# A written order for the first stage of a hybrid decoder block

## The chip, the cores and the metric

The kernel runs on one core of a Trainium2 chip. The metric is the device time of one execution in microseconds (us); lower is better. The engines are TensorE (PE: matmuls, with PEld for its weight loads), VectorE (DVE), ScalarE (ACT), GpSimd (POOL) and SyncE (SP, which here only issues DMAs). Each engine takes its instructions in the order of its own list and waits on semaphores.

## The reference

One decoder block over 1024 tokens of width 1024 in float32. The part that matters here is the beginning:

```python
cond = silu(c)
sh1, sc1, g1, sh2, sc2, g2 = split(cond @ w_ada + b_ada, 6)
h = rmsnorm(x, norm1_g) * (1 + sc1) + sh1
u, q, k, v, gate_a, gate_b = split(h @ w_in)
y_a = s5_branch(u, lam_re, lam_im, log_dt, b_re, b_im, c_re, c_im, d_skip, w_glu, b_glu) @ w_a
y_b = stick_breaking_attention(q, k, v) @ w_b
x = x + g1 * ((sigmoid(gate_a) * y_a + sigmoid(gate_b) * y_b) @ w_o)
# then a second norm and modulation, a SwiGLU FFN of width 2816, and a last norm
```

The S5 branch is a state-space recurrence with complex diagonal states: from `lam`, `log_dt`, `b` and `c` it derives powers of `exp(lam*dt)`, scaled input matrices and output matrices before any token is touched.

## The kernel before, in words

Matmuls with full precision are made of three products: each operand is split into a high half (float32r) and a low half (the rest), and high x high, high x low and low x high are summed (`PRODUCTS`). A weight tile is loaded into a staging tile (`ws` or `wgs`), its high half is cast on ScalarE and its low half is a subtraction on another engine. The halves live in a ring of buffers (`wring`: `wh`/`wl` with two buffers each, used by two of the three entries, and `wgh`/`wgl` with one); `self.turn` counts which entry is next.

The function `start` (L509 to L608) is the first stage. It computes u = h @ w_in[:, 0:512], transposed, in two halves of 512 tokens:

- `load` (L543) fetches four x tiles of 128 tokens and squares them on ScalarE; `half` (L527) computes 1/rms, scales the four tiles (one on ScalarE, one on GpSimd, two on VectorE), transposes them on TensorE column block by column block and copies each block to `xT` on ScalarE.
- `ada(g)` (L552) loads half of the shift and half of the scale columns of w_ada, multiplies them with the conditioning vector on TensorE (`ada_mm`, L860, four products side by side in strips of 32 rows), adds up the strips with a product by ones (L567), and loads and splits two of the four w_in tiles (`u_weight`; low halves on GpSimd, L425).
- `modulate(k, h)` (L575) makes the high half of a modulated column block on ScalarE (L578), the full value on VectorE (L579) and the low half on GpSimd (L580).
- `product` (L589) and `store` (L591): 96 products for each half of the tokens; a store copies a finished block on ScalarE and writes it to `uD` in DRAM. The store buffers `us` are three.
- `small` (L492) loads the small parameter rows on SP's queue and turns them into columns. The class `S5` computes all its parameters in one function, `params` (L78 to L197), on VectorE, with its loads on SP and ScalarE's queue.

After `start` the S5 recurrence (`inject`, `phases`, `outputs`, `run`) runs on VectorE and TensorE beside `v_proj` (L640, product L651) and eight blocks of `gate` (product L630), whose matmuls fill TensorE. `s5.run` waits for u from DRAM. The memory of the first stage's pools is used again by that stage.

The order of instructions on each engine is not written out: a planner (`schedule_with_timeline_sim=True`) simulates the program with its own costs and takes, on each engine, what is ready, earlier program text first. `self.after` and `keep_in_program_order` pin single instructions.

Of the kernel before, what the change touches and what calls it, by code (L numbers as in the profile page):

```python
# [9 lines left out]
F32 = mybir.dt.float32  # L10
F32R = mybir.dt.float32r
# [17 lines left out]
class S5:  # L29


    def __init__(self, tc, pool, work, psum, ident, lam_reT, lam_imT, log_dtT, b_re, b_im, c_re, c_im, d_skip):

        self.tc, self.nc = tc, tc.nc
        self.pool, self.work, self.psum, self.ident = pool, work, psum, ident
        self.params(lam_reT, lam_imT, log_dtT, b_re, b_im, c_re, c_im, d_skip)
# [41 lines left out]
    def params(self, lre, lim, ldt, b_re, b_im, c_re, c_im, d_skip):  # L78
        nc, pool, work = self.nc, self.pool, self.work
        v = nc.vector  # L80
        i = [0]

        def tmp():
            i[0] += 1
            return work.tile([128, 16], F32, name="tmp", bufs=24)
# [4 lines left out]
        tt(th, lim, dt, ALU.mult)  # L90
        self.vexp(r, ar, tmp)
# [5 lines left out]
        reduce(n, th)  # L97

# [8 lines left out]
        tt(w, ph, ph, ALU.mult)  # L107
        ts(s, w, 1.0 / math.factorial(13), None, ALU.mult)
# [6 lines left out]
        ts(c, c, 1.0, None, ALU.add)  # L115
        s2 = an
# [26 lines left out]

        nr, d, zr, zi, q = tmp(), tmp(), tmp(), tmp(), tmp()
# [15 lines left out]
        tt(zi, zi, d, ALU.mult)  # L160

        br, bi, t1, t2 = (work.tile([128, 16, 16], F32, name=k, bufs=1) for k in ("br", "bi", "bt1", "bt2"))
        nc.sync.dma_start(out=br, in_=b_re.rearrange("o (r g) p i -> (o g p) r i", g=2))
        nc.sync.dma_start(out=bi, in_=b_im.rearrange("o (r g) p i -> (o g p) r i", g=2))
# [19 lines left out]
        for srcs, dst in (((c_re, c_im), self.C), ((c_im, c_re), self.Cs)):  # L184
            cl = work.tile([128, 4, 2, 64], F32, name="cl", bufs=2)
            for k, src in enumerate(srcs):
                nc.scalar.dma_start(out=cl[:, :, k], in_=src.rearrange("o (t g) i p -> (o g i) t p", t=4))
# [4 lines left out]
        dsk = pool.tile([32, 16], F32, name="dsk")  # L192
        nc.scalar.dma_start(out=dsk, in_=d_skip.rearrange("o g i -> (o g) i"))
        self.dT = pool.tile([16, 32], F32, name="dT")
        ps = self.psum.tile([128, 512], F32, name="tp")
        nc.tensor.transpose(ps[0:16, 0:32], dsk, self.ident[0:32, 0:32])
# [143 lines left out]
P = 128  # L340
# [55 lines left out]
class Block:  # L396
# [94 lines left out]

    def small(self, const, pp):  # L492

        nc, i = self.nc, self.i
        rows = const.tile([P, P], F32, name="rows")
        ld = const.tile([16, 2], F32, name="ld")
        nc.gpsimd.memset(rows, 0.0)
        for a, n, k in ((64, "b_ada", 48), (48, "norm1_g", 8), (56, "norm2_g", 8), (112, "b_glu", 4)):
            nc.sync.dma_start(out=rows[a:a + k], in_=i[n].rearrange("o (k p) -> (o k) p", p=P))
        nc.sync.dma_start(out=ld, in_=i["log_dt"].rearrange("o (a b) -> (o a) b", b=2))  # L500
        nc.vector.tensor_copy(rows[0:16].rearrange("p (a b) -> p a b", a=2), ld.unsqueeze(2).broadcast_to([16, 2, 64]))
        nc.sync.dma_start(out=rows[16:32], in_=i["lam_re"].rearrange("o (a b) p -> (o a) (b p)", b=2))
        nc.sync.dma_start(out=rows[32:48], in_=i["lam_im"].rearrange("o (a b) p -> (o a) (b p)", b=2))
# [5 lines left out]
    def start(self, const, up, s5p):  # L509

        nc, i = self.nc, self.i
        ss = const.tile([P, KT], F32, name="ss1")
        x_v = i["x"].rearrange("o (t p) d -> p (o t) d", p=P)
        w_v = i["w_ada"].rearrange("o (p k) n -> (o p) k n", k=KT)
        self.hT = [[self.PA.tile([P, 2, 512], F32R, name="pa") for _ in range(KT)], []]
# [912 lines left out]
```

## Time and profile before

| | |
|---|---|
| three runs | 1528.68, 1532.48, 1535.25 us |
| median | 1532.48 us |
| span of the profiled execution, first to last instruction | 1530.4 us |
| TensorE busy in the span | 1409.0 us (92%) |
| VectorE busy | 1072.2 us (70%) |
| ScalarE, GpSimd busy | 614.0 us, 663.2 us |
| end of the last u product | 102.1 us |

The profiled execution's own time is known as its span alone; it lies 2.1 us under the median of the timed runs. In the views below, PE, PEld, DVE, ACT, POOL and SP are engines, a `q` behind a name is its sequencer issuing a DMA, L589 is line 589 of the kernel. A row of a timeline has the start in us, the duration in us, engine, line, operation, output <- input, partitions x elements, a count, and in brackets the idle time before it with what ended it. A row of the chain has start, duration, and engine with line, or a DMA. In the rows by stretches, each engine has busy us and (x instructions); then come TensorE's granted clock, the DMA engines' share and GB/s.

### The profile page before, as it was taken

The numbers are of one execution on the slowest core, as the hardware profiler recorded it, in microseconds if no ns is written. First come the engines' busy times: TensorE is split into PE (matmuls) and PEld (weight loads), VectorE is DVE, ScalarE is ACT, GpSimd is POOL, SyncE is SP. The second block draws the span as 40 slices with busy tenths as digits, with TensorE's granted clock in tenths as the row PEclk, the third lists the DMA queues.
The fourth block names the chain that finished last, engine by engine and source line by source line (L and its number), as shares of the span: only waits on it lengthen the run. The fifth ranks groups of instructions, "written<-read, shape, count | busy, mean of one in ns | idle before, by whom it ended". The sixth has DMA issues, their size and how long they took to land.

```text
span 1530.4 us, 18295 instructions
## 1 busy us (share of the span) xinstructions
PE 1409.0 (92%) x6578; PEld 1107.5 (72%) x6578; DVE 1072.2 (70%) x1443; ACT 614.0 (40%) x800; POOL 663.2 (43%) x369
## 2 busy tenths in 40 slices
PE   4898999996999898969799889999999998999995
PEld 2588888785666565638688668888888887788774
DVE  4658895555677776657624897666666758999998
ACT  5431122712566555655306543333333324343323
POOL 2520000102355557443410126445445459788795
PEclk9899999999999999989899999999999999999998
DMA  8556655498133234227423324333333146555312
GB/s 265 183 136 165 169 141 159 130 287 283 52 114 105 81 99 144 85 96 238 161 101 130 106 69 161 105 106 104 103 104 104 58 145 258 158 159 161 109 54 110
DMA packets 180962, 210.46 MB, mean 138 GB/s; under 512 B 29124, under 2 KB 122408, under 8 KB 180872
## 3 DMA queue, kind: packets, MB, share of 16 engines
q1 hardware_dynamic: 169800, 201.29, 41.5%
q10 hardware_dynamic: 11072, 8.00, 1.8%
q8 instruction: 52, 0.85, 0.2%
q14 instruction: 38, 0.31, 0.1%
HBM read 159.18 MB, written 48.89 MB: 136 GB/s over the span
## 4 chain that ended last, share of the span: by engine, by line
PE 45%; DVE 19%; DMA 12%; issue 10%; POOL 9%; ACT 4%; SPq 1%; ACTq 0%; POOLq 0%; DVEq 0%
PE tq L1143 12%; PE wo L1143 9%; PE wo L1024 5%; PE gu L1143 3%; PE mm L589 3%; PE mm L704 2%; POOL wa L806 2%; PE ga L630 2%; PE mx L704 2%; POOL wh L773 1%; PE mx L630 1%; POOL pb L1203 1%; DMA aw<-in_w_ada_dram 1%; DVE wa L802 1%; DVE acc L875 1%
## 5 line engine op out<-in xcount | busy, mean ns | idle before, releaser
L441 POOL TENSOR_TENSOR ws<-wb 128x1024 f32<-128x1024 f32 x26 | 64.2, 2471 | 192.0 <-PE tq L1046 90.1
L806 POOL TENSOR_TENSOR wa<-wa,wb 128x1024 f32<-128x1024 f32 (+2 forms) x32 | 80.6, 2519 | 73.5 <-DVE wa L802 49.3
L774 DVE TENSOR_TENSOR wl<-ws,wh 128x1024 fp32r<-128x1024 f32 (+1 forms) x40 | 52.7, 1317 | 67.1 <-POOL wh L773 67.1
L425 POOL TENSOR_TENSOR wl<-ws,wh 128x1024 fp32r<-128x1024 f32 x14 | 38.9, 2780 | 136.8 <-ACT wh L422 136.3
L807 ACT ACTIVATE wa<-wa 128x1024 f32<-128x1024 f32 (+1 forms) x40 | 38.9, 971 | 82.2 <-POOL wa L806 81.1
L1196 POOL TENSOR_TENSOR pa<-pa,row 128x1024 f32<-128x1024 f32 x22 | 66.0, 3023 | 1.8 <-DMA pa<-in_w_ffn_down_dram 1.8
L441 POOL TENSOR_TENSOR wgs<-wb 128x1024 f32<-128x1024 f32 x14 | 34.7, 2477 | 73.1 <-DVE wgl L444 30.5
L772 DVE SCALAR_TENSOR_TENSOR ws<-wa,ws 128x1024 f32<-128x1024 f32 (+1 forms) x40 | 53.4, 1335 | 13.0 <-ACT ws L771 12.6
L773 POOL TENSOR_SCALAR wh<-ws 128x1024 fp32r<-128x1024 f32 (+1 forms) x40 | 38.4, 959 | 54.1 <-DVE ws L772 52.8
L1134 POOL TENSOR_TENSOR f<-f,f 128x512 f32<-128x512 f32 x30 | 50.0, 1693 | 26.9 <-DVE f L1124 18.4
L704 PE MATMUL mm<-wa,V 128*64 128x512 f32 (+3 forms) x192 | 40.7, 517 | 21.5 <-ACT wa L807 21.4
L422 ACT CAST wh<-ws 128x1024 fp32r<-128x1024 f32 x28 | 29.2, 1048 | 61.5 <-PE wo L1024 32.9
L769 ACT ACTIVATE ws<-wa 128x1024 f32<-128x1024 f32 (+1 forms) x40 | 38.7, 968 | 30.3 <-DVE wa L766 29.8
L704 PE MATMUL z<-q,k 64*128 64x512 f32 (+3 forms) x192 | 42.6, 535 | 8.9 <-DVE gst L958 8.9
L875 DVE SCALAR_TENSOR_TENSOR acc<-aw,cond,acc 128x512 f32<-128x512 f32 x56 | 43.8, 782 | 9.9 <-DMA aw<-in_w_ada_dram 9.4
L1123 ACT ACTIVATE f<-f 128x1024 f32<-128x1024 f32 x22 | 23.4, 1061 | 60.9 <-DVE f L1163 31.0
L802 DVE TENSOR_TENSOR wa<-wa,acc 128x512 f32<-128x512 f32 (+1 forms) x80 | 46.6, 616 | 1.1 <-PE acc L704 1.1
L1225 POOL TENSOR_TENSOR wb<-pa 128x512 f32<-128x512 f32 x23 | 40.2, 1756 | 15.6 <-DVE wxl L1223 5.5
L273 POOL MEMSET tz<- 128x1024 f32 x4 | 3.8, 953 | 92.8 <-PE s5a L329 84.9
L1134 POOL TENSOR_TENSOR f<-f 128x512 f32<-128x512 f32 x20 | 42.2, 2127 | 0.0
L1242 PE MATMUL wo<-f,f 128*128 128x512 f32 x132 | 40.7, 389 | 0.0
L771 ACT ACTIVATE ws<-ws 128x1024 f32<-128x1024 f32 (+1 forms) x40 | 39.0, 974 | 1.1
(807 smaller groups left out, 4700.7 us busy)
## 6 DMA issues: line engine op xcount, KB each, us to landing
aw<-in_w_ada_dram SPq DMA_DIRECT2D x64, 256.0 KB
wb<-cD SPq DMA_DIRECT2D x32, 512.0 KB
hD<-f SPq DMA_DIRECT2D x30, 512.0 KB
ws<-in_w_in_dram SPq DMA_DIRECT2D x23, 512.0 KB
wb<-in_w_ffn_gate_dram SPq DMA_DIRECT2D x44, 256.0 KB
wb<-in_w_ffn_up_dram SPq DMA_DIRECT2D x44, 256.0 KB
pa<-in_w_ffn_down_dram SPq DMA_DIRECT2D x22, 512.0 KB
wb<-hD SPq DMA_DIRECT2D x40, 256.0 KB
```

The source lines that it names most:

```text
L441: (add or nc.gpsimd).tensor_tensor(st, a, b, op)
L704: return self.tc.keep_in_program_order(self.nc.tensor.matmul(*args, **kw))
L772: nc.vector.scalar_tensor_tensor(st, a, 0.0, st, ALU.max, ALU.add)
L773: nc.gpsimd.tensor_scalar(ht, st, 1.0, 0.0, ALU.mult, ALU.add)
L774: nc.vector.tensor_tensor(lt, st, ht.bitcast(F32), ALU.subtract)
L802: nc.vector.tensor_tensor(a[:, x, 0:f], a[:, x, 0:f], r[:, x, 0:f], ALU.subtract)
L806: nc.gpsimd.tensor_tensor(a[:, :, o], a[:, :, o], behind[:, :, old], ALU.subtract)
L875: nc.vector.scalar_tensor_tensor(acc, w[:, j], cj, acc, ALU.mult, ALU.add)
L1024: nc.tensor.matmul(ps, lhsT=mg[t // 4][k][:, a, P * (t % 4):P * (t % 4) + P], rhs=ws[k // 2][b][:, k % 2], start=(j == 0), stop=(j == 23))
L1134: nc.gpsimd.tensor_tensor(o, a, b, op)
L1143: self.nc.tensor.matmul(ps, lhsT=w[x][:, q, k], rhs=self.B[i](y, k), start=(j == 0), stop=(j == 11))
L1196: nc.gpsimd.tensor_tensor(w, w, g2, ALU.mult)
```

## The change

`start` opens a region in which all five engines keep the order of the program text. In it:

- The modulation is computed in four quarters (each two column blocks of shift and of scale) in place of two halves: w_ada is fetched in pieces of 256 columns, and each quarter's loads, products, sums and modulates follow each other, with the products of the quarter before between them.
- `S5.params` is cut in three: `steps`, a generator whose six pieces of small VectorE instructions are placed between the modulates; `load`, the seven loads, all on SP after the first half's products; and `matrices`, which stands at the end of the stage.
- The small rows are loaded on ScalarE's queue (`rows`) ahead of everything.
- The scaling of x that was on GpSimd goes to VectorE; copies of transposed blocks and of stores alternate between ScalarE and VectorE; the low halves of modulated blocks go to VectorE, except odd blocks of the second half of tokens, which stay on GpSimd.
- The second half's x is loaded ahead of the last quarter of w_ada, and its transposes are done before the first half's last products. The second half's products run block-of-rows first for k = 0 to 3, then output by output.
- Every one of the four w_in tiles counts a turn of the ring; before, the fourth did not.

```diff
-        self.params(lam_reT, lam_imT, log_dtT, b_re, b_im, c_re, c_im, d_skip)
+        self.rows = lam_reT, lam_imT, log_dtT
+        self.given = b_re, b_im, c_re, c_im, d_skip
...
+    def steps(self):            # the body of params, with a yield after
+        # 1: dt, ar, th   2: r, reduce   3: angles   4: sines   5: powers, rho   6: zr, zi
...
+    def load(self):
+        nc.sync.dma_start(out=self.br, in_=b_re.rearrange("o (r g) p i -> (o g p) r i", g=2))
+        nc.sync.dma_start(out=self.bi, in_=b_im.rearrange("o (r g) p i -> (o g p) r i", g=2))
+        # four loads of c_re and c_im, one of d_skip, all on nc.sync
+    def matrices(self):         # bbr, bbi, bst, A, B, C, Cs, dT as in params
...
+                self.tc.manual_schedule(engines={E.PE, E.Activation, E.DVE, E.Pool, E.SP}):
...
+            def u_load(a):
+                self.turn += 1
+                ring = self.wring[a] if a < 3 else (ap, "u3h", "u3l", self.wring[0][3], "ws", 2)
+                pool, ht, lt, spool, stag, sbufs = ring
+                w = spool.tile([P, 1024], F32, name=stag, bufs=sbufs)
+                nc.sync.dma_start(out=w.rearrange("p (k n) -> p k n", n=512), in_=u_v[:, 2 * a:2 * a + 2, 0:512])
...
+            def u_split(a):
+                nc.scalar.copy(h, w)
+                nc.gpsimd.tensor_tensor(l, w, h.bitcast(F32), ALU.subtract)
...
+            def ada_load(g):
+                for q in range(2):
+                    for a in range(2):
+                        w = self.PB.tile([P, 4, 256], F32, name="pb")
+                        n = 1024 * q + 256 * g
+                        self.last_ada = nc.sync.dma_start(out=w, in_=w_v[:, 4 * a:4 * a + 4, n:n + 256])
...
+                    (nc.vector.tensor_copy if k % 2 else nc.scalar.copy)(xT[:, k, 512 * h:512 * h + 512], q)
...
-                nc.gpsimd.tensor_tensor(t[:, 1], xk, t[:, 0].bitcast(F32), ALU.subtract)
+                    (nc.gpsimd if h and k % 2 else nc.vector).tensor_tensor(t[:, 1], xk, t[:, 0].bitcast(F32), ALU.subtract)
...
+                self.upin = (nc.vector.tensor_copy if m % 2 else nc.scalar.copy)(u, acc[m].rearrange("p (c j) -> p j c", j=8))
...
+            self.rows(const)
             load(0)
+            u_load(0)
+            ada_load(0)
+            u_load(1)
+            ada_load(1)
+            squares(0)
...
+            next(steps)
+            scale(0)
+            turned(0, range(KT))
+            u_split(0)
+            ada_products(0)
+            ada_sums(0)
+            for g in range(4):
+                k = 2 * g
+                modulate(0, (k, k + 1))
+                if g < 3:
+                    u_split(g + 1)
+                if g == 0:
+                    u_load(2)
+                    ada_load(2)
+                    u_load(3)
+                    load(1)
+                if g == 1:
+                    ada_load(3)
+                next(steps)
+                if g == 2:
+                    squares(1)
+                    scale(1)
+                    product(0, (k, k + 1), range(4))
+                    ada_products(3)
+                    turned(1, range(4))
+                    ada_sums(3)
+                    modulate(0, (6, 7))
+                    turned(1, range(4, KT))
+                    break
+                product(0, (k,), (0, 1))
+                ada_products(g + 1)
+                product(0, (k,), (2, 3))
+                ada_sums(g + 1)
+                product(0, (k + 1,), range(4))
+            modulate(1, (0, 1))
+            product(0, (6,), range(4))
+            for m in range(4):
+                product(0, (7,), (m,))
+            s5.load()
+            for m in range(4):
+                store(0, m)
+            for k in range(4):
+                product(1, (k,), range(4))
+                modulate(1, (k + 2,))
+                if k < 2:
+                    next(steps, None)
+            modulate(1, (6, 7))
+            next(steps, None)
+            for m in range(4):
+                product(1, range(4, KT), (m,))
+                store(1, m)
+            s5.matrices()
```

More of the change, by code (lines that the diff above doesn't have):

```diff
@@ L76, in cmul, with tmp @@
         tt(di, di, t2, ALU.add)
[L78 to L85, printed above, removed]
+    def tmp(self):
+        return self.work.tile([128, 16], F32, name="tmp", bufs=24)
+    def steps(self):
+        pool, work, tmp = self.pool, self.work, self.tmp
+        lre, lim, ldt = self.rows
+        v = self.nc.vector
         tt, ts, stt = v.tensor_tensor, v.tensor_scalar, v.scalar_tensor_tensor
@@ L183, in params @@
         self.Cs = pool.tile([128, 32, 16], F32, name="Cs")
[L184 to L187, printed above, removed]
+        for cl, dst in zip(self.cl, (self.C, self.Cs)):
             ps = self.psum.tile([128, 512], F32, name="tp")
@@ new lines, in product, with store @@
+            def product(h, ks, ms):
+                for k in ks:
+                    for m in ms:
+                        for n, (a, b) in enumerate(PRODUCTS):
+                            nc.tensor.matmul(acc[m], lhsT=ws[k // 2][a][:, k % 2, P * m:P * m + P], rhs=self.hT[h][k][:, b], start=k + n == 0, stop=k + n == KT + 1)
+            def store(h, m):
+                u = up.tile([P, 8, 64], F32, name="us", bufs=3)
+                self.upin = (nc.vector.tensor_copy if m % 2 else nc.scalar.copy)(u, acc[m].rearrange("p (c j) -> p j c", j=8))
+                nc.sync.dma_start(out=self.uD[P * m:P * m + P, :, 64 * h:64 * h + 64], in_=u)
@@ L607, in start @@
             self.hT[1] = [self.PB.tile([P, 2, 512], F32R, name="pb") for _ in range(KT)]
+            modulate(1, (0, 1))
+            product(0, (6,), range(4))
             for m in range(4):
-                store(m, 0, acc[m])
-            half(1)
-            for k in range(KT):
-                modulate(k, 1)
+                product(0, (7,), (m,))
+            s5.load()
             for m in range(4):
-                q = (mp, self.mm, self.mm, mp)[m].tile([P, 512], F32, name="mm")
-                for k in range(KT):
-                    product(q, m, k, 1)
-                store(m, 1, q)
+                store(0, m)
@@ L620, in in_cols @@
+            acc = [(mp, self.mm, self.mm, mp)[m].tile([P, 512], F32, name="mm") for m in range(4)]
+            for k in range(4):
[9 more added lines that the diff above has]
+            s5.matrices()
     def in_cols(self, c0):
```

161 lines of the change are left out of this document (84 added, 77 removed).

## The prediction

> **What bounds the kernel now.** I read the busy times by stretches first, then the chain of work that ended last, then the instructions of each engine in the first 103 us.
>
> ```profile
> core 0: us, PE busy (x) PEld busy (x) DVE busy (x) ACT busy (x) POOL busy (x), PEclk, DMA share, GB/s
> 0.00:15.00 15.00, 0.18 (x1) 0.18 (x1) 0.84 (x5) 7.37 (x11) 0.85 (x7) 1.00 0.61 183
> 15.00:43.00 28.00, 21.43 (x106) 12.33 (x105) 22.97 (x119) 14.06 (x22) 10.78 (x5) 0.82 0.99 331
> 43.00:57.07 14.07, 14.06 (x72) 9.71 (x72) 9.67 (x25) 5.09 (x8) 6.38 (x4) 1.00 0.92 336
> 57.07:64.30 7.23, 2.38 (x16) 1.64 (x12) 4.79 (x11) 5.90 (x10) 3.52 (x2) 0.88 0.15 55
> 64.30:102.10 37.80, 37.80 (x171) 31.22 (x172) 13.62 (x14) 16.99 (x26) 15.36 (x11) 0.93 0.26 62
> ...
> 102.10:250.00 147.90, 142.66 (x981) 126.40 (x980) 129.81 (x288) 27.30 (x52) 4.07 (x8) 0.98 0.60 154
> 250.00:350.00 100.00, 97.88 (x445) 80.65 (x445) 50.61 (x63) 42.95 (x53) 6.74 (x7) 1.00 0.71 217
> ```
>
> The first stage ends at 102.10. TensorE has next to nothing until 15, works in pieces until 43, stands for most of 57.07 to 64.30 and is full afterwards. It stays nearly full until 350 (240.54 of 247.9 us), so what the stage gains at its end can reach the end of the kernel, if TensorE stays fed. VectorE is the second bound there: 129.81 of 147.90 us up to 250.
>
> ```profile
> 2.50 9.42 DMA cl<-in_c_im_dram
> 11.94 0.25 SPq L499
> ...
> 18.00 11.44 DMA ws<-in_w_in_dram
> ...
> 32.23 0.96 PE tp L190 x4
> ...
> 41.21 1.76 POOL pa L580
> 43.01 3.06 PE mm L589 x12
> ...
> 62.59 1.67 POOL pa L580
> 64.30 5.36 PE mm L589 x12
> 69.66 0.87 PE tp L540 x8
> ...
> 89.70 12.41 PE mm L589 x54
> 102.10 6.32 DMA uD<-us
> ```
>
> The chain says what the start waits for: SP's small loads stand behind a slow load of c_im until 11.94, w_ada and w_in follow, and GpSimd's low halves (L580) hold TensorE at 43 and again at 62.59. From 64.30 on the chain is TensorE alone.
>
> **The change, part by part.** I work out when the u products start, what TensorE then has to do, where it waits, and what comes after its last product.
>
> ```profile
> 21.90 8.63 SPq L164 DMA_DIRECT2D bi<-in_b_im_dram  x1
> ...
> 11.60 1.06 ACT L550 ACTIVATE xT<-x 128x1024 f32<-128x1024 f32 x1 [0.25 <-DMA x<-in_x_dram]
> 14.82 0.45 PE L506 MATMUL tp<-ident,rows 128*128 128x128 f32 x1 [14.82 <-DMA rows<-in_lam_im_dram]
> 22.56 1.43 DVE L63 SCALAR_TENSOR_TENSOR tmp<-tmp 128x16 f32<-128x16 f32 x7
> 24.84 1.92 ACT L541 COPY xT<-tp 128x512 f32<-128x512 f32 x3 [0.27 <-PE tp L540]
> 26.12 3.64 PE L860 MATMUL tp<-pb,cond 128*32 128x512 f32 x32
> 40.58 0.53 DVE L579 TENSOR_SCALAR xT<-xT,G,mod 128x512 f32<-128x512 f32 x1
> 54.38 0.95 PE L567 MATMUL adap<-ones,acc 128*128 128x1 f32 x8
> 60.94 2.20 DVE L536 TENSOR_SCALAR x<-x,ry 128x1024 f32<-128x1024 f32 x2
> 212.01 0.68 DVE L304 TENSOR_TENSOR scr<-scr 128x512 f32<-128x512 f32 x1
> ```
>
> Start. The last x tile lands at about 11.5 now, beside the c loads that the change takes away from here; four tiles of 512 KB at the 331 GB/s of the second stretch need 6.3 us, so 9.5 to 11.5; I take 10. Its square (1.06; 1.3 with its sum and the hop, an estimate) ends at 11.3. The small rows go to ACT's queue and no longer wait 14.82 us; the first S5 piece (18 small VectorE instructions at 0.2, from 1.43/7: 3.6 us) now stands ahead of rstd on VectorE and ends about 12. Rstd as an estimate of 1.5 us: 13.5. Three scalings on VectorE at 0.6 to 1.1 (2.20/2, beside a GpSimd scaling that they no longer have): 2 us, 15.5. The eight transposed columns had a pitch of some 0.85 with ACT alone copying (two copies and their waits); with VectorE taking every second one I take 0.65: 20.7. One quarter of the modulation is half of 3.64: 1.8, so 22.5. Copy, four sums (0.95), the two small VectorE instructions: 2.4, so 24.9. The first modulate: ACT, 0.53, then the low half on VectorE (0.68 by the nearest row): 2.1. The u products start at **27**, against 43. If w_ada lands late, with 1 KB pieces in place of 2 KB, 31 is the other end; 25 if nothing slips.
>
> TensorE's work from there: 192 products at 0.23 (12.41/54), 44.1; three quarters at 1.8, 5.5; their sums, 3 x 0.95 = 2.9; the second half's transposes, 4 x 0.87 = 3.5. **56.0** us. Now the same stretch takes 59.1 (43.01 to 102.10), so nearly all that can be gained is the earlier start.
>
> ```profile
> 37.28 2.36 POOL L425 TENSOR_TENSOR wgl<-wgs,wgh 128x1024 fp32r<-128x1024 f32 x1 [1.63 <-ACT wgh L422]
> 37.31 2.36 DVE L157 TENSOR_TENSOR tmp<-lpi,cols 128x16 f32<-128x16 f32 x1
> 99.36 1.29 ACT L593 COPY us<-mm 128x512 f32<-128x512 f32 x2 [0.77 <-PE mm L589]
> 103.29 0.59 ACT L593 COPY us<-mm 128x512 f32<-128x512 f32 x1 [0.23 <-DMA uD<-us]
> ```
>
> Stalls. In a written order each engine waits where its list says. The pair of rows in which a tiny VectorE instruction lasts exactly as long as GpSimd's split shows that the one locks the other out; three of the four splits of w_in fall beside VectorE work here.
> - Per quarter VectorE has two modulates (2.4), a piece (4.2, then about 2.8) and the sums' end (0.4), then 1.2 for the next k: 6.8 to 8.2, and up to 2.4 more behind GpSimd. TensorE has 24 products, a quarter and its sums: 8.2. So 0 to 2.4 each; 1.5 for both.
> - x's second half: 5.2 MB (w_in, a quarter, w_in, x) at 331 GB/s behind the first 7.3 MB, landed near 42; four squares, rstd and scaling till 50 to 52; TensorE gets there at about 50. Two (0 to 4).
> - The last four transposed columns wait for copies that stand behind modulates in the lists of ACT and VectorE: 2.5 (0 to 4).
> - Second half: the fourth store waits for the first one's buffer, as it does now (copied by 99.95, landed by 103.2: 3.3 us), but it now stands on VectorE ahead of the modulate of k=2 and of two pieces (29 and 15 small instructions, some 3.8 and 2.4). TensorE has two k ready (5.5 us) and then waits for k=3 and for 4 to 7: 3 (0 to 6).
> - The clock: 12 products took 5.36 behind the stop at 57 to 64, where 2.76 is the full rate: 2.6 lost. TensorE also comes out of a sparse stretch here: 2.5 (0 to 5).
>
> Sum 11.5 (0 to 21). The stage's last product ends at 27 + 56.0 + 11.5 = **94.5**, against 102.1: 7.6 earlier. With its ends, 85 to 105.
>
> [...]
>
> ```profile
> 50.30 0.43 DVE L71 TENSOR_TENSOR bt<-bi,tmp 128x256 f32<-128x256 f32 x1
> 52.24 0.59 DVE L177 COPY bst<-bbi 64x256 f32<-64x256 f32 x2
> 98.63 1.23 DVE L425 TENSOR_TENSOR wgl<-wgs,wgh 128x1024 fp32r<-128x1024 f32 x1 [0.86 <-ACT wgh L422]
> 102.71 0.07 DVE L205 MEMSET tc<- 128x16 f32 x1 [2.86 <-PE mm L589]
> 139.78 0.58 PE L651 MATMUL mm<-wl,pa 128*128 128x256 f32 x1 [4.70 <-DVE wl L425]
> 244.97 1.40 DVE L320 TENSOR_TENSOR h<-scr 64x508 f32<-64x508 f32 x2
> 252.09 0.39 PE L329 MATMUL s5a<-u,tz 128*128 128x128 f32 x2
> ```
>
> After the last product. The S5 matrices (18 VectorE instructions and three groups of transposes) ran in gaps and now stand behind the last store. Six complex products at 0.34 and twelve copies at about 0.27: 5.2 us of VectorE. So the next stage's VectorE work, which begins at 102.71 now, begins at 94.5 + 0.7 + 5.2 = 100.4: 2.3 earlier where TensorE is 7.6 earlier. What covers the difference of 5.3: at the end of the S5 work VectorE is done at 246.4 and TensorE reaches its use at 252.09, 5.7 later. So nothing for it, 5.2 if that cover is gone. The nine transposes (0.96 for four) cost TensorE 1.0 there; they were beside waits.
>
> The seven S5 loads move from SP and ACT at the start to SP, ahead of the first stores. One of them held SP for 8.63 us. Nothing makes them wait but SP's place behind the last quarter's load, about 37 us in, so they should be out and landed before the first store near 66: nothing; up to 9 us on a store, and through the fourth store on VectorE, if they are issued late.
>
> The weight ring moves on by one, since every u load counts a turn. The second v_proj weight now falls into the single wg buffer, free only when the last group has used it (about 1.4 before the end). Cast, then its low half (1.23 on VectorE): no wait if VectorE takes it ahead of the matrices, 5 if behind; the nearest row is the 4.70 at 139.78, the same wait for a v_proj low half. I take 1.5.
>
> **Sum.** 7.6 - 1.0 - 1.5 = 5.1 us off the span of 1530.4: 1525.3. The median of the three runs is 1532.48, 2.1 above that span; carried over, **1527.4**.
>
> **The rivals.**
> - Few stalls (B). The order was written for these engines' lists; if VectorE keeps pace and only the clock and 2 or 3 us of waits remain, the stage ends at 27 + 56 + 5 = 88; 14 earlier, less 2.5 and less what VectorE lags beyond its cover (1): 1522. For it: in the second stretch VectorE's 22.97 us are mostly S5 pieces that would now be spread. Against it: the lock, and a fourth store on VectorE.
> - VectorE is the bound of the next stage (C); this is the one on the slower side. TensorE's 142.66 of 147.90 stands beside VectorE's 129.81, and the 4.70 wait shows TensorE waiting for VectorE there. Then the kernel's end moves with VectorE's start: 2.3 earlier at best by my sum, and it decides as soon as the stage ends later than 96.8 (96.8 + 5.9 = 102.7). At 102 it starts 5.2 late: 1537.7. Against it: the 5.7 us of cover. [...]
> - The written stage only changes the plan of the rest (D): ring and ready times differ, so the planner orders the S5 stage and the gates anew. Bounds from the 4.70 wait, gained or had twice, on top of the sum: 1518 to 1537.
>
> **How the numbers follow.** My forecast (A), a stage that ends between 91 and 98: 0.42, 1527.4, own range 1522 to 1533. B 0.28, C 0.18, D 0.12. Half a per cent, what a measurement of this kernel can tell, is 7.7 us: under 1524.8, over 1540.1. Faster: 0.08 of A, 0.28, 0.04 of D: 0.40. Slower: 0.08 of C and 0.06 of D, both with the late end of my bounds (105): 0.14. Same: 0.46. The range takes in B and most of C: 1514 to 1538.
>
> **What would show it.** Right: the first L589-like product between 25 and 31; no TensorE stop over 3 us from there to the last u product; that product at 91 to 98; VectorE's memset of tc about 6 us later; TensorE full up to 250. Wrong: the u products starting after 33 (w_ada late), GpSimd splits and VectorE waits adding to more than 15 us of stops, a TensorE wait of 5 us for a v_proj weight, or a stage that ends where I say while the next one gives the time back.

## The result, and the profile after

| | before | changed |
|---|---|---|
| median of five runs each | 1532.48 us | 1543.77 us |
| lowest, highest | 1528.68, 1538.05 | 1542.82, 1544.54 |
| ratio, 95% interval | 1 | 1.0078 (1.0052 to 1.0103) |
| span of the profiled execution | 1530.4 us | 1542.5 us |
| first u product | 38.8 us | 32.0 us |
| last u product ends | 102.6 us | 107.7 us |
| VectorE's memset of tc (next stage begins) | 102.7 us | 115.8 us |

The change makes the kernel 11.3 us slower. 1527.4 was forecast, and the time lies 5.8 above the upper end of the range, 1538. The u products start earlier, as forecast, and then take 75.7 us in place of 63.8. (The 102.1 us given for before further up is where its chain passes from TensorE to a store's load; the last product itself ends at 102.6. The line numbers of the changed kernel: L589 of before is L632, L205 is L226, L329 is L350, L651 is L740.)

The first view is again the busy time by stretches; the third and fourth rows are the u stage from its first to its last product, of the changed kernel and of before.

```profile
0.00:15.00 15.00, 0.45 (x1) 0.18 (x1) 1.90 (x10) 7.04 (x11) 0.86 (x7) 1.00 0.86 292
15.00:32.00 17.00, 9.85 (x72) 6.81 (x72) 7.92 (x28) 6.29 (x11) 2.35 (x1) 1.00 0.82 272
32.00:107.70 75.70, 64.98 (x346) 47.84 (x347) 51.24 (x146) 28.81 (x43) 13.09 (x7) 0.91 0.52 145
...
250.00:350.00 100.00, 91.10 (x401) 74.13 (x400) 50.43 (x72) 41.17 (x51) 6.40 (x7) 0.93 0.57 173
```

```profile
38.80:102.60 63.80, 58.40 (x272) 44.36 (x271) 32.28 (x67) 29.21 (x46) 27.86 (x19) 0.92 0.45 144
```

From its first u product to its last TensorE is busy for 64.98 of 75.70 us: 10.7 idle, and 9.0 busy beyond the 56.0 that its products should take. The granted clock says what most of the 9.0 is; the next rows cut the stage finer.

```profile
32.00:40.00 8.00, 7.47 (x42) 3.99 (x43) 7.41 (x22) 2.19 (x3) 2.37 (x1) 0.58 1.05 382
40.00:70.00 30.00, 25.30 (x179) 19.00 (x178) 22.95 (x61) 14.88 (x24) 4.80 (x2) 0.99 0.62 170
70.00:73.00 3.00, 2.33 (x10) 1.73 (x9) 1.92 (x4) 2.00 (x3) 0.00 (x0) 0.50 0.00 0
73.00:76.00 3.00, 3.00 (x9) 2.33 (x8) 1.66 (x4) 0.00 (x0) 1.17 (x1) 0.50 0.00 0
```

TensorE's clock is 0.58 for 8 us at the start and 0.50 for 6 us at 70: (1 - 0.58) x 8 + 0.5 x 6 = 6.4 us, a little less in truth, since TensorE also stood for 1.2 us in them. Between 250 and 350 TensorE is busy for 91.10 us, where it was busy for 97.88 before, again at a lower clock (0.93 against 1.00). That is the second place in which time is lost, and one row of the timeline has it:

```profile
264.06 0.77 PE L350 MATMUL s5a<-u,tz 128*128 128x128 f32 x2 [6.22 <-DMA gD<-gst]
```

TensorE stands for 6.22 us at the last block of the S5 products, a wait that before does not have. The transfer named there only came last by the record; the operand is `tz`, and VectorE's chain to it reads:

```profile
246.89 1.43 DVE L276 TENSOR_TENSOR o<-C,A 128x576 f32<-128x576 f32 x2 [5.13 <-PE s5a L351]
...
257.27 0.27 DVE L292 TENSOR_TENSOR rt<-rt,dd 16x128 f32<-16x128 f32 x1
...
257.62 3.46 SPq L297 DMA_DIRECT2D tz<-rt  x4
...
260.79 1.40 DVE L341 TENSOR_TENSOR h<-scr 64x508 f32<-64x508 f32 x2
```

```profile
241.45 0.27 DVE L271 TENSOR_TENSOR rt<-rt,dd 16x128 f32<-16x128 f32 x1
...
241.80 3.51 SPq L276 DMA_DIRECT2D tz<-rt  x4
...
252.09 0.39 PE L329 MATMUL s5a<-u,tz 128*128 128x128 f32 x2
```

VectorE makes the output matrices `o`, TensorE multiplies with them, VectorE finishes `rt`, eight loads bring it into `tz` (the row shows the four on SP's queue; four more are on ScalarE's), and 6.4 us after their first issue (257.62 to 264.06) TensorE can go on. In before that chain is issued at 241.80, so its operand is there at about 248.2, and TensorE comes for it at 252.09. It is 15.8 us later now, and VectorE's stage began 13.1 later. The 2.7 us between the two are a wait of VectorE: ahead of this `o` it stands 5.13 us for TensorE's S5 products of the block before (first row above), and 2.40 in before:

```profile
231.08 1.43 DVE L255 TENSOR_TENSOR o<-C,A 128x576 f32<-128x576 f32 x2 [2.40 <-PE s5a L330]
```

So the two engines wait for each other there.

### The profile page after: what moved, and what is told of

It is laid out like the page before. It is cut to its first block, busy times and chain, and to the rows that moved or that the text cites. A ratio compares the mean times of both kernels' runs of the same rounds, so it can differ in the third digit from the quotient of the medians.

```text
span 1542.5 us, 18427 instructions
## 1 busy us (share of the span) xinstructions
PE 1415.5 (92%) x6642; PEld 1110.9 (72%) x6642; DVE 1094.7 (71%) x1473; ACT 606.8 (39%) x788; POOL 642.8 (42%) x355
## 4 chain that ended last, share of the span: by engine, by line
PE 26%; DVE 11%; issue 7%; POOL 6%; DMA 1%; ACT 1%; DVEq 0%; POOLq 0%; ACTq 0%
PE tq L1232 10%; PE wo L1232 8%; PE wo L1113 5%; PE gu L1232 3%; POOL pb L1292 1%; POOL wb L1314 1%; DVE f L1316 1%; POOL pa L1285 1%; DMA hD<-f 1%; DVE wl L1312 1%; DVE pb L1337 1%; DVE x L1337 1%; POOL f L1223 1%; POOL x L1292 1%; DVE f L1312 1%
## 5 line engine op out<-in xcount | busy, mean ns | idle before, releaser
L446 POOL TENSOR_TENSOR wl<-ws,wh 128x1024 fp32r<-128x1024 f32 x12 | 33.5, 2789 | 119.0 <-ACT wh L443 104.8
L896 ACT ACTIVATE wa<-wa 128x1024 f32<-128x1024 f32 (+1 forms) x40 | 38.8, 971 | 81.2 <-POOL wa L895 81.2
L443 ACT CAST wh<-ws 128x1024 fp32r<-128x1024 f32 x24 | 25.2, 1048 | 63.3 <-PE wo L1113 35.1
```

## The experiments

Two theories were to be told apart first. V: the S5 stage is set by VectorE from its memset of tc on (a stretch of 143.7 us in before, 146.4 changed), so the kernel's end follows VectorE's start. T: the end follows TensorE's last u product (some of the expectations call it P). A third, D, is the rival of the prediction: the plan of all that lies behind the stage. The table has one profiled execution of each kernel (us from the start) and the median of the runs; the same written stage ends anywhere between 106.7 and 109.3 in it, so a difference of 2 us in these columns says little; "stretch" is from the memset of tc to VectorE's last h, "attention" is its first product.

| kernel | last u product | memset of tc | stretch | last h | attention | median | ratio to before (95%) |
|---|---|---|---|---|---|---|---|
| before | 102.6 | 102.7 | 143.7 | 246.4 | 382.8 | 1532.5 | 1 |
| changed | 107.7 | 115.8 | 146.4 | 262.2 | 394.6 | 1543.8 | 1.0078 (1.0052 to 1.0103) |
| mat_early | 106.5 | 107.9 | 142.1 | 249.9 | 386.8 | 1538.2 | 1.0045 (1.0028 to 1.0062) |
| rstd_first | 103.7 | 111.8 | 144.7 | 256.5 | 386.6 | 1534.8 | 1.0017 (0.9997 to 1.0037) |
| planned | 96.1 | 97.4 | 145.8 | 243.2 | 381.4 | 1533.5 | 1.0011 (0.9995 to 1.0027) |
| delay_before | 102.9 | 103.5 | 152.7 | 256.2 | 391.1 | 1537.5 | 1.0028 (1.0011 to 1.0045) |
| turn_before | 102.5 | 102.6 | 144.3 | 246.9 | 379.3 | 1529.8 | 0.9990 (0.9971 to 1.0009) |
| turn_after | 107.6 | 115.7 | 145.7 | 261.4 | 400.2 | 1545.4 | 1.0096 (1.0065 to 1.0128) |
| turn_planned | 97.1 | 98.4 | 144.5 | 242.9 | 384.8 | 1530.9 | 1.0002 (0.9986 to 1.0018) |
| turn_both | 104.3 | 105.6 | 142.4 | 248.0 | 384.9 | 1535.7 | 1.0023 (1.0005 to 1.0041) |
| before_light | 103.1 | 103.3 | 128.0 | 231.3 | 373.9 | 1521.7 | 0.9929 (0.9914 to 0.9944) |
| after_light | 107.0 | 115.1 | 132.4 | 247.5 | 382.3 | 1530.8 | 0.9988 (0.9972 to 1.0005) |
| planned_light | 95.3 | 96.7 | 134.5 | 231.2 | 369.2 | 1519.4 | 0.9910 (0.9895 to 0.9925) |
| planned_moved | 97.0 | 98.3 | 119.4 | 217.7 | 366.6 | 1547.3 | 1.0092 (1.0069 to 1.0114) |
| before_te | 102.9 | 103.1 | 122.5 | 225.6 | 423.0 | 1568.9 | 1.0242 (1.0219 to 1.0265) |
| planned_te | 96.2 | 97.5 | 121.0 | 218.5 | 406.0 | 1558.8 | 1.0179 (1.0157 to 1.0200) |
| after_te | 106.7 | 114.8 | 118.5 | 233.3 | 423.2 | 1572.7 | 1.0267 (1.0248 to 1.0286) |
| both_te | 103.5 | 104.9 | 120.4 | 225.3 | 416.6 | 1567.8 | 1.0220 (1.0195 to 1.0245) |
| after_sc | 109.3 | 117.3 | 138.9 | 256.2 | 386.3 | 1534.6 | 1.0008 (0.9995 to 1.0022) |
| planned_sc | 95.4 | 96.7 | 140.5 | 237.2 | 378.4 | 1530.7 | 0.9996 (0.9985 to 1.0008) |

**mat_early: the S5 matrices ahead of the last products.**

```diff
+            s5.matrices()
             for m in range(4):
                 product(1, range(4, KT), (m,))
                 store(1, m)
-            s5.matrices()
```

> The changed kernel with the S5 matrices placed ahead of the last group of u products instead of behind the last store. Theory V (the end of the kernel follows the moment at which VectorE begins the recurrence, the memset of tc: 102.7 us before, 115.8 after): VectorE has idle time from 97 to 107 there, the memset comes at 109 to 110, and the kernel ends some 6 us earlier than the changed one, near 1538. Theory P (the end follows TensorE's last u product, 5.1 us later than before, and the rest is replanning): the last product does not come earlier, so 1543 to 1545.

The last u product moves by 1.2 us, no more than it varies, and VectorE's start by 7.9; the kernel gains 5.6. That is V's number, and the wait of 6.22 us is gone.

**rstd_first: the scaling of x ahead of the S5 pieces.**

```diff
-            next(steps)
             scale(0)
+            next(steps)
...
-                next(steps)
                 if g == 2:
                     squares(1)
                     scale(1)
+                next(steps)
```

> The changed kernel with rstd and the scaling of x ahead of the S5 piece that stands beside them, in both halves (the first piece, and the sines). Both theories: the u products start 3 to 4 us earlier (28.5), TensorE's stop before the second half's transposes shrinks by about 4, and the stage ends 4 to 6 us earlier (102 to 104). V: the memset of tc at 110 to 112, the kernel at 1538 to 1540. P: the same size. If the rest of the plan alone counts (theory D), no steady answer: within 2 us of 1543.8.

The first u product comes 2.3 us earlier (29.7), the last one 4.0, VectorE's start 4.0. The kernel gains 9.0, which is more than either theory had: 8 of it are there at the start of the attention, 5.7 at the last h. The 6.2 us wait is still there in it, so the wait alone is not the whole loss.

**planned: the text of the change, without the written order.**

```diff
-                self.tc.manual_schedule(engines={E.PE, E.Activation, E.DVE, E.Pool, E.SP}):
+                ExitStack():
```

> The changed kernel's text, quarters, pieces and engine choices, but without the written order: the planner orders the stage. It tells the order from the new parts. V: the matrices go into VectorE's gaps, the memset of tc comes within 2 us of the last u product, and the kernel ends at 1530 to 1536. If the quarters and the moved work are what costs, it stays at 1540 or later.

Here the stage does what was forecast: the last u product ends at 96.1, 6.5 earlier than in before, and VectorE starts 5.3 earlier. The kernel ends level with before. At the last h 3.2 us of it are left, at the start of the attention 1.4.

**delay_before: VectorE alone delayed, in the kernel before.**

```diff
+        v.memset(tc_, 0.0)
+        for _ in range(5):
+            v.tensor_tensor(tn[:, :, 0:64], tc_[:, :, 0:64], tc_[:, :, 0:64], ALU.mult)
         v.memset(tc_[:, :, 0:1], 1.0)
```

> The kernel before with VectorE work added where the phases begin: one memset and five products of 128x1024 into tn, about 7 us in all, which change no result. V: the kernel ends 6 to 8 us later, 1538 to 1541. P: TensorE is nearly full there and reached the last S5 products 5.7 us after VectorE was done, so at most 2 us: 1532 to 1535.

The last u product stays; the stretch grows by 9.0 us and the kernel by 5.3 over the runs of before beside it (1532.17). TensorE gets the wait that the changed kernel has:

```profile
254.29 1.19 PE L332 MATMUL s5a<-u,tz 128*128 128x128 f32 x4 [8.39 <-DMA tz<-rt]
```

So work added to VectorE alone puts TensorE to wait there. T, which had at most 2 us, does not explain 5.3 (interval 1.7 to 6.9), but V's 6 to 8 is not reached either: some 4 of the 9 us are taken back behind it.

**The ring's fourth turn: turn_before, turn_after, turn_planned, turn_both.** Before gets one more turn, or the changed kernel one fewer; turn_both has both repairs of above too.

```diff
-                self.turn += 1
+                self.turn += a < 3
```

> The kernel before with one turn more on the weight ring behind its four u loads, as the change has it, and nothing else. The first stage stays (last u product at 102 to 103). Theory V (the end follows VectorE's start): no change, within 1.5 us of before. Theory D (the stages behind are planned anew, and that moves the end by some us whatever the first stage does): a shift of 2 to 5 us to either side that begins behind 250 us.

> The changed kernel without the fourth turn: the second v_proj weight falls into the two-buffer entry again. My term for this was 1.5 us (0 to 5). V: the low half that stood ahead of the matrices on VectorE goes elsewhere, the memset of tc 1 to 1.5 us earlier, the end 1 to 2 us earlier than the changed kernel: 1542. D: a few us to either side.

> The changed text ordered by the planner, without the fourth turn. With the turn its stage ended 6.5 us earlier than before and the memset of tc came 5.3 earlier, yet the kernel ended level. If the ring's phase is what took the gain: 1526 to 1528. If it is replanning of another kind, or a bound further on: 1531 to 1534 again.

> The written order with both mends (matrices ahead of the last group of products, rstd ahead of the S5 piece) and without the fourth turn. V: last u product near 103, the memset of tc at 103 to 105, TensorE no longer waits for the last recurrence, and the kernel ends within 2 us of before: 1531 to 1535. If the written order costs by something else than VectorE's start, 1536 or later.

With the turn, before is not measurably different (0.9971 to 1.0009); without it the changed kernel is no faster (1545.4) and planned stays level. The ring's phase is neither the loss nor what takes planned's gain. In turn_both VectorE starts at 105.6 and 8 of the 11 us are back, so most of the loss lies in two places of the written order. The two repairs do not add: rstd_first alone gained 9.0. And 1535.7 lies just above the 1531 to 1535 expected.

**before_light, after_light, planned_light: VectorE relieved.** Beside the S5 work VectorE multiplies four columns of the modulation, 32 operations. These kernels leave out 496 of the 512 columns of each, so they do not compute the block and only measure. These groups of before are VectorE's costliest in that stretch:

```profile
L875 DVE SCALAR_TENSOR_TENSOR acc<-aw,cond,acc 128x512 f32<-128x512 f32 x28 | 20.8, 744 | 6.3 <-DMA aw<-in_w_ada_dram 6.2
L310 DVE TENSOR_TENSOR_SCAN scr<-rho,scr 128x128 f32<-128x128 f32 x32 | 10.9, 402 | 0.1
L320 DVE TENSOR_TENSOR h<-scr 64x508 f32<-64x508 f32 x16 | 10.9, 680 | 0.3
L425 DVE TENSOR_TENSOR wl<-ws,wh 128x1024 fp32r<-128x1024 f32 x7 | 8.5, 1215 | 0.0
```

```diff
-                    nc.vector.scalar_tensor_tensor(acc, w[:, j], cj, acc, ALU.mult, ALU.add)
+                    nc.vector.scalar_tensor_tensor(acc[:, c], w[:, j, c], cj, acc[:, c], ALU.mult, ALU.add)
...
+                c = slice(0, 16 if n < 8 else 512)
```

> The kernel before, with the four columns of the modulation that VectorE computes beside the S5 work (acc<-aw, 32 operations, 22.7 us in the trace of before between 98 and 262) cut to 16 of their 512 columns; their loads stay. Theory V (VectorE's work sets the end of the S5 stretch): the stretch from the memset of tc to the last h, 143.7 us in before, loses most of the 19 us that are left out, and the last h ends near 230; TensorE, which had 5.2 idle us in that stretch, is then the bound, and the kernel gains up to about 5 us: 1526 to 1530. Theory D (what lies behind the S5 stretch takes and gives the difference): the last h ends as early, and the kernel ends at 1532, as before.

> The changed kernel with the same cut. Theory V: VectorE starts 13.1 us later than in before but has 19 us less to do, so TensorE's wait of 6.2 us at the last S5 products and the low clock behind it go; the kernel falls from 1543.8 to between 1531 and 1536, and what is left between it and the kernel before with the same cut is the later last u product, 5.1 us or less. Theory T (the loss is TensorE's alone, its last u product 5.1 us late plus what the plan adds): 1539 to 1543, still 11 us over the kernel before with the same cut.

> The text of the change without the written order (its last u product 6.5 us earlier than in before, its time level with before), with the same cut. Theory V: the gain of the first stage was lost because VectorE's stretch did not shorten with it; with VectorE relieved the last u product's 6.5 us show, less 2 us of waits for weights: 4 to 6 us under the kernel before with the same cut, 1521 to 1525. Theory D (the chain of loads behind the S5 stretch takes it): within 2 us of the kernel before with the same cut.

With the cut the changed kernel loses 13 us and the kernel before 10.8, and TensorE's stop at the last S5 products is gone from the changed one. Its stretches:

```profile
100.00:250.00 150.00, 148.31 (x1018) 130.93 (x1017) 124.80 (x314) 29.56 (x55) 4.08 (x8) 1.00 0.59 154
250.00:300.00 50.00, 47.34 (x222) 38.81 (x221) 19.62 (x21) 30.40 (x35) 4.88 (x2) 1.00 0.60 177
```

```profile
100.00:250.00 150.00, 148.71 (x1032) 131.94 (x1031) 118.41 (x294) 32.06 (x59) 4.07 (x8) 1.00 0.67 171
250.00:300.00 50.00, 50.00 (x223) 41.39 (x222) 23.91 (x26) 32.44 (x39) 5.70 (x5) 1.00 0.45 144
```

TensorE is busy for 198.7 of 200 us in before_light; in before it was 192.6 (144.76 and 47.88 in the same two stretches). So VectorE's work bounded both kernels there, and the 5 us that I had expected of before was too little: 6.1 us of TensorE's idle time came back, and with it the clock (1.00 over 150 us where before had 0.98, 3 us). What I had expected of after_light came true (1531 to 1536, measured 1530.8), but not the difference that was to be left: 9.1 us between the two, where V as I had put it leaves 5. About 4 of these are TensorE's later start (107.0 against 103.1) and 3 its shorter busy time in the rows above (195.65 against 198.71); the rest I have not placed. In planned_light the earlier stage shows at last, but with 2.3 of its 7.8 us, under the 4 to 6 expected and nearer to D's 2: TensorE waits more in it while the stretch runs (145.16 of 150 busy).

**planned_moved: the four columns computed in the attention instead.** `ada_rest(4 + m, ...)` is taken out of the S5 loop and eight halves of 256 columns stand between the units of the attention, each four loads into `gst` buffers, eight VectorE operations and a store.

> The text of the change without the written order, with the whole computation: the four columns of the modulation are computed in the attention instead, in eight halves of 256 columns, through the two gst buffers, 64 VectorE operations of 128x256 (about 0.4 us each, an estimate from 0.74 for 128x512: 26 us). In the attention VectorE is busy for about 70% of the time (263.4 us of 385 between 385 and 770 in before). Theory V: the S5 stretch gains as in the kernel with the cut, and the attention hides the 26 us: 1521 to 1528. If the attention does not hide them, or the two buffers hold up the gate products: 1540 and more.

The S5 stretch falls to 119.4 and the attention starts at 366.6, 16 us before that of before. Then the attention takes 404.2 us from its first product to the first of w_o, where it took 370.8: it does not hide the VectorE work (26 us by the estimate above), though VectorE is busy for 70% of it in before. One stretch of each shows it:

```profile
430.00:480.00 50.00, 41.77 (x179) 25.77 (x178) 43.30 (x48) 25.81 (x29) 24.51 (x17) 0.96 0.46 143
530.00:580.00 50.00, 40.69 (x179) 26.20 (x177) 44.31 (x52) 21.90 (x26) 27.86 (x19) 0.97 0.45 135
```

```profile
430.00:480.00 50.00, 46.38 (x210) 29.45 (x210) 38.07 (x41) 30.99 (x35) 29.59 (x21) 1.00 0.37 116
530.00:580.00 50.00, 47.91 (x223) 31.37 (x221) 37.64 (x42) 29.99 (x35) 32.24 (x22) 1.00 0.29 90
```

VectorE goes from 76 and 75% to 87 and 89%, TensorE from 46.38 and 47.91 to 41.77 and 40.69. Whether VectorE's time itself or the two shared buffers hold TensorE is not told apart.

**before_te, planned_te, after_te, both_te: the four columns on TensorE.** The products are `ada_mm`, as in the first stage, in text behind the first four gates; the result is copied from PSUM by ScalarE. both_te has the two repairs.

```diff
-                if k + j == 0:
+                if n < 8:
+                    self.ada_mm(ps, k + j, w[:, j])
+                elif k + j == 0:
```

> The kernel before, with the four columns of the modulation of the S5 stretch multiplied on TensorE as the first stage does it (four products side by side, 32 products of 128x512 in all; 3.64 us for as many in the trace of before), each copied from PSUM by ScalarE, behind the first four gates in the program's text. Nothing is left out. Theory V: VectorE's stretch loses 22.7 us, as much as with the cut (1521.7), and TensorE gets some 4 us more work and its idle time back: 1524 to 1528, under before by 0.3 to 0.5%. Against V: if the cut gained by what it left out of the loads' waits or elsewhere, or if the PSUM banks that wait for these loads hold up the gate products: 1530 and more.

> The text of the change without the written order, with the same move to TensorE. Theory V with what the cut showed: 2 us under before_te (1519.4 against 1521.7 with the cut), so 1522 to 1526.

> The changed kernel with the same move. Theory V: 1533 to 1537, 7 to 11 us under the changed kernel and 9 over before_te, as with the cut (1530.8 against 1521.7), because TensorE's last u product is 4 to 5 us later and its idle time behind the stage is not gone. Theory T (TensorE's lateness alone counts, 5 us): 1530.

> As the one before, with the matrices ahead of the last products and the scaling of x ahead of the S5 pieces (the two repairs together, with the ring's fourth turn): VectorE's S5 stretch begins at about 105.6 instead of 115.8 and the last u product ends at about 104: 1526 to 1531, within 3 us of before_te if the stage's end is all that the written order lost.

All four lose 25 to 36 us against the kernels without the move (both_te against turn_both, which has a turn less), and not at the S5 stretch, which is down to 118.5 to 122.5. The groups of TensorE in before_te say where:

```profile
L860 PE MATMUL mm<-aw,cond 128*32 128x512 f32 x32 | 16.8, 747 | 10.8 <-DMA aw<-in_w_ada_dram 10.8
L860 PE MATMUL mx<-aw,cond 128*32 128x512 f32 x28 | 9.4, 605 | 0.0
```

Each of these float32 products stands as two records in the trace (in the first stage of before 64 for 32 products), so the 32 are 64 records, of which 60 are here. They keep TensorE busy for 26.2 us, 0.44 per record, in twos and fours as the loads bring them through two buffers, for which TensorE stands 10.8 us more. In the first stage of before, where sixteen come together, a row reads:

```profile
55.26 1.92 PE L860 MATMUL tp<-pb,cond 128*32 128x512 f32 x16
```

That is 0.12 per record. A single record lasts at least 0.59 us in both places; what differs is how many overlap. My expectation was wrong twice: the row of 3.64 us holds half of what four columns need (32 of 64 records), and it comes from a place where the operands are all there. All four expectations were missed. TensorE's 37 us in before_te (26.2 and 10.8) outweigh whatever VectorE's shorter stretch gave, so these runs say nothing for V or against it, and give no faster kernel.

**after_sc, planned_sc: 7.2 us of copies from VectorE to ScalarE.** The eight vst copies (0.41) and six gst copies (0.68) of the S5 stretch. The edit also moves two gst copies behind 262 (at 280.86 and 298.68); nothing else.

```diff
-            if h:
-                nc.vector.tensor_copy(st, ps)
-            else:
-                nc.scalar.copy(st, ps)
+            nc.scalar.copy(st, ps)
...
-                (nc.vector.tensor_copy if t % 2 else nc.scalar.copy)(v, ps[:, 0:256])
+                nc.scalar.copy(v, ps[:, 0:256])
```

> The changed kernel, with the eight vst copies (0.41 us) and the six gst copies (0.68 us) that VectorE makes between 97 and 262 given to ScalarE, which is busy for 27.9 of 150 us there: 7.2 us off VectorE, nothing left out. Theory V: the stretch from the memset of tc to the last h falls from 146.4 by 5 to 7, TensorE's wait of 6.2 us at the last S5 products goes, and the kernel from 1543.8 to between 1535 and 1539. Theory T: TensorE's lateness is the loss, and nothing changes by more than 2 us: 1542 to 1545.

> The text of the change without the written order, with the same copies on ScalarE. Theory V: planned stood level with before although its stage ends 6.5 us earlier; with 7.2 us off VectorE, and the cut of 19 us worth 14 (1533.5 to 1519.4), 3 to 5 us: 1528 to 1531. Otherwise 1532 to 1535.

after_sc is the clearest run. The written order and its late stage stay (last u product 109.3, VectorE's start 117.3), the stretch shrinks by 7.5, and the kernel by 9.1, a little more than V expected, to no measurable difference from before. TensorE's wait, which V expected to go, is still there, but smaller:

```profile
258.64 0.77 PE L350 MATMUL s5a<-u,tz 128*128 128x128 f32 x2 [3.70 <-DMA gD<-gst]
```

```profile
100.00:250.00 150.00, 148.85 (x1017) 131.51 (x1018) 127.04 (x286) 34.56 (x68) 4.22 (x9) 1.00 0.59 156
250.00:300.00 50.00, 44.22 (x201) 35.80 (x200) 19.02 (x24) 27.68 (x33) 2.38 (x1) 0.97 0.59 169
```

TensorE is busy for 193.1 us of these 200, against 187.65 in the changed kernel (146.55 and 41.10), with a clock of 1.00 and 0.97 where it had 0.99 and 0.88. Might the move have helped by freeing the banks of PSUM (where a gate product stands until its copy to `gst`) sooner, and not by relieving VectorE? In the changed kernel no wait of TensorE between 108 and 300 is put down to a copy out of PSUM: it stands 6.2 us ahead of `tz` (the row above), 2.8 for `o`, 2.6 for `yp` and 0.5 for a weight. Sixteen copies moved make up for what the order cost; before with the same copies moved was not run, so this does not say that the 9.1 us are the order's alone. planned_sc's 1530.7 is as expected (1528 to 1531), but no measurable gain over before (0.9985 to 1.0008); no version that computes everything and measurably beats before was found.

**How VectorE's lateness becomes TensorE's wait.** While VectorE works at a block of the S5 stage, TensorE has gate products to do: 48 for each gate, 288 for the six gates whose loads the text does not put behind the last S5 product (`s5.last_mm if m >= 6`). In before TensorE has 76 of them left between its S5 products of the last two blocks, and does not wait. In the changed kernel 30 are left, all 288 are done, and it waits 6.22 us. The other runs agree: 72 left in mat_early and in planned, no wait; 41 in after_sc, 3.70; 30 in rstd_first, 6.2; 5 in delay_before, 8.39. Where the blocks stand in TensorE's list is the planner's choice, and each edit made it plan the rest anew. So it is shown that work put on VectorE or taken off it there moves the end (delay_before, after_sc, the cut); how much of that is VectorE's own time and how much the blocks' new places is not told apart.

## Why the prediction was wrong

The forecast was A, a stage end between 91 and 98; what came is nearest to rival C, given 0.18: VectorE bounds the next stage, and "it decides as soon as the stage ends later than 96.8". VectorE's next stage was forecast to begin at 100.4 and began at 115.8, 15.4 later; the time is 16.4 over the forecast. C's rule, that the end moves with VectorE's start, gives 1545.6 with the 13.1 us by which it came later than in before, 1.8 off. As a rule it is too simple: planned starts VectorE 5.3 earlier and gains nothing, rstd_first 4.0 earlier than the changed kernel and gains 9.0. Three steps of the sum failed, and one reading under them.

**Start: 27 forecast, 32.0 measured.**

```profile
8.13 0.32 ACTq L523 DMA_DIRECT2D rows<-in_lam_im_dram  x1
...
13.05 0.45 PE L531 MATMUL tp<-ident,rows 128*128 128x128 f32 x1 [13.05 <-DMA rows<-in_lam_im_dram]
13.54 0.29 DVE L532 COPY cols<-tp 128x128 f32<-128x128 f32 x1 [9.86 <-PE tp L531]
...
17.27 0.16 DVE L474 TENSOR_SCALAR rv<-ss 128x4 f32<-128x4 f32 x1
...
18.73 2.08 DVE L611 TENSOR_SCALAR x<-x,ry 128x1024 f32<-128x1024 f32 x3
...
19.93 7.09 PE L617 MATMUL tp<-ident,x 128*128 128x128 f32 x32 [6.43 <-ACT x L609]
```

The squares are done at 12.8, but the rows, issued on ScalarE's queue only at 8.13, land at 13.05. S5's first piece waits for them and rstd (the 1/rms of x) waits behind the piece until 17.27, where 12 was forecast for its start. The piece itself (3.4 us) and the scalings (2.08) were sized right. That single place is the 5 us: from there to the first u product 15.0 us were forecast and 14.7 measured. rstd_first starts rstd at 13.29, 4.0 earlier, but only 2.3 of it reach the first product (29.7), because the piece then holds up VectorE's copies of the transposed columns (the first at 20.14). I had costed the piece by its length, and not asked when its own input lands: of a step put ahead in a list, what it waits for counts as well as what it does. The 43 that the 27 was set against was misread too; four u products of before run earlier:

```profile
38.80 2.08 PE L589 MATMUL mm<-pa,wh 128*128 128x512 f32 x4
```

So the start gained 6.8 us and not 11, and the stretch to compare with was 63.8 us and not 59.1.

**Stalls: 11.5 forecast, 19.7 measured** (10.7 idle and 9.0 over the 56.0 of TensorE's work). The waits were near (9.0 forecast without the clock): 0.8 for the pairs with the split (1.5 forecast), 2.7 for the second half's x (2), 2.5 for the transposed copies (2.5), 4.8 in the second half's products (3). These rows are the lock and the waits:

```profile
33.68 2.37 POOL L569 TENSOR_TENSOR wl<-ws,wh 128x1024 fp32r<-128x1024 f32 x1 [3.39 <-ACT wh L568]
33.76 2.83 DVE L626 TENSOR_TENSOR pa<-xT,pa 128x512 fp32r<-128x512 f32 x1
```

```profile
60.35 0.16 DVE L474 TENSOR_SCALAR rv<-ss 128x4 f32<-128x4 f32 x1
...
81.44 0.69 DVE L636 COPY us<-mm 128x512 f32<-128x512 f32 x1 [2.36 <-DMA uD<-us]
```

```profile
63.02 0.60 PE L617 MATMUL tp<-ident,x 128*128 128x128 f32 x3 [2.32 <-ACT x L609]
...
69.42 1.12 PE L617 MATMUL tp<-ident,x 128*128 128x128 f32 x4 [1.54 <-ACT xT L618]
...
90.34 0.50 PE L632 MATMUL mm<-pb,wh 128*128 128x512 f32 x1 [2.16 <-POOL pb L626]
...
98.63 0.50 PE L632 MATMUL mm<-pb,u3h 128*128 128x512 f32 x1 [1.60 <-POOL pb L626]
```

VectorE's low half of 0.69 us lasts 2.83 beside GpSimd's split, three times in the stage (2.83 to 2.88). The sines stood ahead of rstd of the second half; the fourth store waited for its buffer (2.36), and the low halves on GpSimd came late behind it (2.16 and 1.60). The term that was mis-sized most is the clock: 2.5 forecast for one ramp, 6.4 measured in two, the first behind single waits of at most 1.36 us since 19.93 (the longest before 32.01), the second behind a stretch in which none was longer than 2.32 us. The clock stood at 0.50 from 70 to 76, behind stops of 2.32 (before 63.02) and 1.54 (before 69.42), while behind the longer one of 6.43 before 19.93 it was 1.00 from 20 to 30. In before, too, the stop "at 57 to 64" of the forecast was in pieces, the longest the 2.63 of this row, and the clock stood at 0.50 from 64.30 to 68:

```profile
64.30 0.80 PE L589 MATMUL mm<-pa,wgh 128*128 128x512 f32 x1 [2.63 <-POOL pa L580]
```

What makes it fall is open. From 60.69 to 71.98 TensorE had only transposes and eight small sums, with stops between them; but the stop of 2.16 us before 90.34, among products, left the clock at 1.00.

So the last product ended at 107.7 and not 94.5: 5.0 from the start, 1.7 of waits, 6.5 of TensorE's busy time beyond the 2.5 forecast for the clock. Of the 6.5 the clock is 3.9; of the other 2.6 a part is the second half's transposes, which came in six groups and kept TensorE busy for 5.9 us, some of it at the low clock, where 3.5 was charged.

**After the last product: charged at nothing, by a cover that was gone.** The matrices were forecast at 5.2 us and took 6.1, with a weight's low half (1.23 at 107.22) ahead of the last store; VectorE began 8.1 after the last product where 5.9 was forecast. I had named the cover (5.7 us, "5.2 if that cover is gone"), and read it off the wrong event: TensorE's wait is for `tz`, whose chain over VectorE and the loads was ready at about 248.2 in before (an estimate: 241.80 and the 6.4 of above), not for VectorE's end at 246.4, and to 252.09 that leaves 3.9. More than that, 5.7 was slack for a stage whose TensorE comes as early as forecast; once TensorE's start had slipped by 5.1 and VectorE's by 13.1, 8.0 of relative lateness stood against 3.9, which is 4.1 of the 6.2 measured. mat_early gives back 7.9 of VectorE's lateness, and 5.6 us of the time.

**The other terms.** The ring and v_proj at 1.5: 0.5, a single wait for a low half; TensorE goes from the last u product through the transposes (1.04) into v_proj without a wait (108.32), and the turn runs agree. The seven S5 loads: zero, as forecast. Rival D has some right: planned ends its stage 6.5 us early and gives all of it back before the end, so even the stage that A forecast might have been worth nothing by itself. Part of that is VectorE's wait for TensorE ahead of the last `o`, 6.6 us in planned where before has 2.40. That a stage gained is time gained was the assumption under the sum ("what the stage gains at its end can reach the end of the kernel, if TensorE stays fed"); VectorE's 129.81 of 147.90 us, with another 6.2 us of waits for loads, left little room for that, and the cut shows it: with less VectorE work TensorE is busy for 198.7 of 200 us. GpSimd's lock on VectorE came as read from the two rows of 2.36 us in before: VectorE's 2.83 beside GpSimd's 2.37, ending 0.54 us behind it (36.59 and 36.05).

**What stays open.** rstd_first gained 9.0 with 4.0 at VectorE's start. The time from the last S5 product to the attention's first varies between 122 and 133 us among these kernels (planned_moved and the four on TensorE left out; 127 in before) and takes or gives up to 6 us that I have not traced to one cause.

## What to carry to other kernels

Before an earlier stage is counted as time gained, find the engine that the next stage waits for last, and take that engine's start, not TensorE's; here both theories of the loss looked alike until VectorE alone was delayed, and relieved. An operation placed in a written order costs what its own input makes the engine wait, and everything behind it in the list pays: here the rows landed at 13.05, and rstd stood behind the S5 piece until 17.27. And look how much work the other engine has left for the time that it must wait (76 products and no wait, 30 and 6.22 us). A few copies moved to an engine with time to spare (9.1 us) were worth nearly what the reordering cost (11.3).

## What was not expected of the hardware

The 128x512 products of the modulation, in strips side by side, take 1.92 us for 16 records when they come together (0.12 each), and 0.44 each on average when they come in twos and fours, though one lasts at least 0.59 in both; the price of one is no property of the instruction alone. From the first issue of the eight loads of `tz` to TensorE's use 6.4 us pass. TensorE's clock fell to 0.50 (70 to 76) behind a stretch with no stop over 2.32 us, and stayed at 1.00 (20 to 30) behind one of 6.43.
